# Second MLP, block 0: the first product done classically throughout, and the raw weights of the seven-product groups kept in two tiles that are loaded by quarters

## The chip, the cores and the metric

The kernel runs on one core of a Trainium2 chip. The metric is the device time of one execution in microseconds, as the median of several runs. One further execution was profiled; all rows below are from it.

## The reference

One inference step of a two-layer network on 640 tokens (512 latent and 128 context tokens) of width 1024. Each layer is a token mixer (pooling in layer 0, retention in layer 1) followed by a squared-ReLU MLP of hidden width 4096:

```python
def sq_relu_mlp(h, w1, w2):
    return jnp.square(jax.nn.relu(h @ w1)) @ w2

for i in range(DEPTH):                       # DEPTH = 2
    ...
    x = x + g_a * mix
    h = rmsnorm(x, norm_mlp_w[i]) * (1 + sc_m) + sh_m
    x = x + g_m * sq_relu_mlp(h, mlp_w1[i], mlp_w2[i])
```

The change touches `h @ w1` of both MLPs. All of it is float32.

## The kernel before, in words

**Precision.** A float32 matrix is split into two parts, high and low (`split`: ScalarE casts the high part, VectorE subtracts to get the low part). Each product is three matmuls (`mm3`): high by high, high by low, low by high. Activations lie transposed, 128 channels by 640 tokens per tile; a matmul takes 320 tokens, half of them. Tiles `h0h` to `h7l` are the MLP's input in its parts, `a` the hidden activations, `whi` and `wlo` the parts of weights, `wst` the raw weights as loaded. There are two buffers `wst` of 1024 KB and four pairs `whi`, `wlo`, so that splitting runs a few products ahead of TensorE.

**Blocks.** `mlp(i, ...)` goes over four blocks `b` of 1024 hidden channels. Each block is a first product (`h @ w1` for these channels, then ReLU, square, split: `hidden`) and a second product (`w2`, added into `x` by VectorE: `add_to_x`). In the second product, and in the classical first product, each of 8 column groups `n` takes 2 halves of tokens by 8 k-tiles by 3, 48 matmuls, 384 in all.

**Seven products.** For the blocks in `FAST` the first product is done in two halves of 512 columns, each by seven products of quarter matrices in place of eight (`fast`): 7 by 2 by 4 by 3, 168 matmuls in place of 192. The generator `seven` loads the raw weights of a half in two transfers of 1024 KB, makes the sums of weight quarters on VectorE (in place in `wst`) and yields seven split operands. The results gather in the PSUM banks `u`, `c11` and `c21`; bank `u` is used four times, and before TensorE may add the next product into it, ScalarE (`S.copy`) or VectorE (`kept`) must have read it.

**Sums of the activations.** The seven products need sums of quarters of the activations too: `quarters()` makes them, for each q of 4, with 12 VectorE instructions and 4 ScalarE casts on tiles of 128 by 320. They go to the tiles `tq`, and one of them overwrites the second half of tokens of `h0` to `h3`. It can therefore run only when no classical product needs these any longer. With `FAST[i] = (1, 2, 3)` the first MLP calls it at the start of block 1. In the second MLP `PART` has it run in block 0: there the columns 0 to 511 are done classically (`follow`, along with the norm that makes `h`), and the columns 512 to 1023 by seven products.

**Order.** The program is written in the order of the stages. A scheduler then merges the instructions of neighbouring stages into one fixed list for each engine (PE TensorE, DVE VectorE, ACT ScalarE, SP the queue that issues the loads), and each engine goes through its list strictly in order. A transfer is issued when its buffer is free of readers.

Of the kernel before, what the change touches and what calls it, by code (L numbers as in the profile page):

```python
# [9 lines left out]
F32 = mybir.dt.float32  # L10
# [55 lines left out]
PART = (False, True)  # L66
# [47 lines left out]
def hybrid_kernel(ctx: ExitStack, tc: tile.TileContext, x_prompt, x_sample, state_ret, c, c_ctx, w_ada, b_ada,  # L114
# [632 lines left out]
    def mlp(i, sq, norm, hm, step, along):  # L747

        with tc.tile_pool(name=f"hid{i}", bufs=1) as hid:
# [17 lines left out]
            def quarters():  # L767

                both = [hid.tile([128, 2048], F32, tag="both", name=nm("tq"), bufs=4).bitcast(F32R) for _ in range(4)]
                place = lambda q, t: [both[q][:, (2 * t + e) * HALF:(2 * t + e + 1) * HALF] for e in range(2)]  # L770
                part = lambda d, h: [z[:, HALVES[h]] for z in hm[d]]
                for q in range(4):
                    b11, b12, b21, b22 = (th() for _ in range(4))
                    for f, (d, h) in ((b12, (q, 1)), (b22, (q + 4, 1)), (b11, (q, 0)), (b21, (q + 4, 0))):
                        hi, lo = (z.bitcast(F32) for z in part(d, h))
                        V.tensor_tensor(f, hi, lo, ALU.add)
                    V.tensor_tensor(b22, b12, b22, ALU.subtract)
                    split(b22, *place(q, 1))
                    V.tensor_tensor(b12, b11, b12, ALU.subtract)
                    split(b12, *part(q, 1))  # L780
                    V.tensor_tensor(b11, b22, b11, ALU.subtract)
                    split(b11, *place(q, 0))
                    V.tensor_tensor(b21, b11, b21, ALU.add)
                    split(b21, *place(q, 2))
# [5 lines left out]
            def seven(src):  # L790


                (a11, a12), (a21, a22) = ([st[:, 4 * e:4 * e + 4] for e in range(2)] for st in (
                    load(src[:, o:o + 256], (8, 256)) for o in (0, 256)))
# [6 lines left out]
                yield split(a12, *parts())  # L801
# [3 lines left out]
                V.tensor_tensor(a12, a12, a11, ALU.add)  # L805
                V.tensor_tensor(a11, a11, a22, ALU.subtract)
                yield split(a11, *parts())
                yield split(a21, *parts())
                yield split(a12, *parts())
                yield split(a22, *parts())  # L810

            def fast(src, half, ops, take):

                ws = seven(src[:, half * 512:(half + 1) * 512])
# [30 lines left out]
            def fast_to_x(src, half, ops):  # L845


                ws = seven(src[:, half * 512:(half + 1) * 512])
                banks = {}

                def put(n, h, ps, gate):
                    t = th()
                    for j, cols in PARTS[h]:
                        S.activation(t[:, cols], ps[:, cols], AF.Copy, scale=gate[:, n, j:j + 1])
                    nc.gpsimd.dma_start(out=away[n][h], in_=t, accum_op=ALU.add)

                w = next(ws)
                for p, name in enumerate(("u", "c11", "u", "c21", "u", "u", "c21")):
                    after = next(ws, None)
                    for t in range(2):  # L860
# [7 lines left out]
                        put(*((n, 0), (n, 0), (n + 2, 0), (n + 2, 1), (n + 2, 1), (n, 1), (n + 2, 0))[p], ps,  # L868
                            minus if p in (2, 4) else mod[i][5])
                    w = after  # L870

            if BOTH[i]:
                away = [[dram.tile([128, HALF], F32, name=nm("away")) for _ in range(2)] for _ in range(KD)]
                minus = const.tile([128, KD, 2], F32, name="minus")
                V.tensor_scalar(minus, mod[i][5], -1.0, None, ALU.mult)

            def hidden_quarters():
# [6 lines left out]
                def places():  # L884
# [6 lines left out]
                    return ([[a[q + o][h] for q in range(4)] for o, h in ((0, 0), (4, 0))] +  # L891
                            [[sums[q, t] for q in range(4)] for t in range(2)] +
                            [[a[q + o][h] for q in range(4)] for o, h in ((0, 1), (4, 1))] +
                            [[sums[q, 2] for q in range(4)]])

                kept, have = {}, set()
                full = lambda z: z.bitcast(F32)

                def less(z, parts, op=ALU.subtract):

                    out = th()
                    for part in parts:
                        V.tensor_tensor(out, z, full(part), op)
# [3 lines left out]
                def take(n, h, ps):  # L907
# [10 lines left out]
                    if n < 4 and (q, 0) in have and (q, 1) in have:  # L918
# [4 lines left out]
                        else:  # L923
                            V.tensor_tensor(t, full(a[q][0][0]), f, ALU.subtract)
                            V.tensor_tensor(t, t, full(a[q][0][1]), ALU.add)
# [17 lines left out]
            for b in range(4):  # L943
# [29 lines left out]
                if b in FAST[i] or b == 0 and PART[i]:  # L973
                    if b == (0 if PART[i] else FAST[i][0]):
                        ops = quarters()
                    for half in range(b == 0, 2):
# [4 lines left out]
                    if b not in BOTH[i]:  # L981
                        get(2 * b + 1, 0)
                else:
                    for n in range(4 if b == 0 else 0, 8):
                        if n == FREE:
                            room[0] = room[1]
                        for h in range(2):
                            hidden(n, h, gemm([get(2 * b, n)], hm, h)[0])
                        step(STEPS[b][0][n])
# [388 lines left out]
```

## Time and profile before

| what | us |
|---|---|
| median of 3 runs | 1642.67 (1642.53 to 1644.59) |
| the profiled execution, its own time | 1642.23 |
| its span, first to last instruction | 1640.5 |
| TensorE busy in the span | 1585.3 (97%) |
| VectorE busy | 1175.7 (72%) |
| ScalarE busy | 730.3 (45%) |

1.7 us of the profiled execution lie around the span. Busy shares are means over stages with different limits, so they are to be read together with the idle time of TensorE by place.

### The profile page before, as it was taken

The page shows a single profiled execution, that of the slowest core. Times are in us where ns is not written, and L with a number is a line of the kernel's source. Part 1 is how long each engine was busy: PE and PEld are TensorE (multiplying, and loading weights), DVE is VectorE, ACT ScalarE, POOL GpSimd, SP SyncE. Part 2 cuts the span into 40 slices and gives each one's busy share as a digit, 9 for nine tenths or more (in the row PEclk, how much of TensorE's full clock was granted, in tenths as well). Part 3 has the DMA queues.
Part 4 walks back from the last instruction along what each step waited for, and adds up shares of the span by engine and source line. Part 5 has one row for each costly group of instructions (what it writes and reads, how often), then busy time and mean ns, then how long its engine had stood idle before and what let it go on. Part 6 is the DMA issues. An engine that isn't in the chain of part 4 may idle for free.

```text
span 1640.5 us, 24467 instructions
## 1 busy us (share of the span) xinstructions
PE 1585.3 (97%) x9873; PEld 1475.0 (90%) x9873; DVE 1175.7 (72%) x2267; ACT 730.3 (45%) x1347; POOL 11.9 (1%) x26
## 2 busy tenths in 40 slices
PE   6999999999999989999999999999969999999997
PEld 3559999999999978899889988989869999999997
DVE  7879996676765887875877688688885464554654
ACT  6747337246165354423432533353464272451640
POOL 0000000000000000000000000000000000000000
PEclk9999999999999999999999999999979999999999
DMA  9744233333314123233423332331104032131221
GB/s 358 240 153 142 93 101 114 104 117 103 103 52 155 56 78 120 87 104 102 131 75 114 94 102 77 128 112 66 56 1 129 27 121 86 52 103 52 92 77 65
DMA packets 137953, 169.81 MB, mean 104 GB/s; under 512 B 3512, under 2 KB 111472, under 8 KB 137840
## 3 DMA queue, kind: packets, MB, share of 16 engines
q1 hardware_dynamic: 134800, 161.28, 29.9%
q0 software_dynamic: 1312, 4.20, 0.8%
q10 hardware_dynamic: 1728, 2.78, 0.5%
q8 instruction: 77, 1.26, 0.3%
q14 instruction: 36, 0.29, 0.1%
HBM read 161.43 MB, written 6.82 MB: 103 GB/s over the span
## 4 chain that ended last, share of the span: by engine, by line
PE 79%; DVE 10%; ACT 5%; DMA 4%; issue 1%; ACTq 0%; DVEq 0%; SPq 0%; POOLq 0%
PE ps L212 22%; PE ps L213 22%; PE ps L214 22%; PE ps L287 3%; DMA wst<-in_mlp_w_dram 3%; PE ps L1124 2%; PE ps L1122 2%; PE ps L1123 2%; DVE wlo L152 2%; ACT whi L151 2%; DVE acc L393 1%; PE ps L635 1%; DMA wst<-in_ret_w_in_dram 1%; PE ps L469 1%; ACT t L487 0%
## 5 line engine op out<-in xcount | busy, mean ns | idle before, releaser
L151 ACT CAST whi<-wst 128x1024 fp32r<-128x1024 f32 x248 | 256.6, 1046 | 436.9 <-PE ps L213 222.3
L152 DVE TENSOR_TENSOR wlo<-wst,whi 128x1024 fp32r<-128x1024 f32 x248 | 300.3, 1221 | 127.1 <-ACT whi L151 127.0
L212 PE MATMUL ps<-a,whi 128*128 128x320 f32 x896 | 277.0, 310 | 1.4 <-ACT a L151 1.4
L213 PE MATMUL ps<-a,whi 128*128 128x320 f32 x896 | 277.3, 310 | 0.1
L214 PE MATMUL ps<-a,wlo 128*128 128x320 f32 x896 | 276.2, 309 | 0.0
L504 DVE SCALAR_TENSOR_TENSOR xall<-ps,mod,xall 128x320 f32<-128x320 f32 (+2 forms) x288 | 115.5, 435 | 170.3 <-PE ps L214 169.2
L213 PEld LDWEIGHTS ps<-a,whi 128*128 128x128 f32 x896 | 168.2, 188 | 2.3 <-DVE a L152 1.9
L212 PEld LDWEIGHTS ps<-a,whi 128*128 128x128 f32 x896 | 167.9, 188 | 1.9 <-ACT a L151 1.8
L214 PEld LDWEIGHTS ps<-a,wlo 128*128 128x128 f32 x896 | 168.0, 188 | 0.0
L393 DVE SCALAR_TENSOR_TENSOR acc<-wst,c,acc 128x256 f32<-128x256 f32 x336 | 137.1, 477 | 0.0
L212 PE MATMUL ps<-tq,whi 128*128 128x320 f32 x312 | 97.6, 313 | 15.3 <-issue 13.5
L213 PE MATMUL ps<-tq,whi 128*128 128x320 f32 x312 | 97.2, 312 | 0.0
L214 PE MATMUL ps<-tq,wlo 128*128 128x320 f32 x312 | 96.9, 312 | 0.0
L213 PE MATMUL ps<-A,whi 128*128 128x320 f32 x256 | 79.1, 310 | 0.0
L212 PE MATMUL ps<-A,whi 128*128 128x320 f32 x256 | 79.1, 312 | 0.0
L214 PE MATMUL ps<-A,wlo 128*128 128x320 f32 x256 | 78.4, 310 | 0.0
L212 PEld LDWEIGHTS ps<-tq,whi 128*128 128x128 f32 x312 | 59.4, 190 | 15.8 <-issue 13.7
L152 DVE TENSOR_TENSOR a<-t,a 128x320 fp32r<-128x320 f32 x128 | 61.7, 487 | 15.8 <-ACT a L151 15.5
L439 ACT ACTIVATE t<-xall 128x320 f32<-128x320 f32 x56 | 25.9, 470 | 84.1 <-DVE xall L504 84.0
L956 ACT ACTIVATE t<-t 128x320 f32<-128x320 f32 x128 | 60.4, 472 | 1.7
L213 PEld LDWEIGHTS ps<-tq,whi 128*128 128x128 f32 x312 | 59.4, 191 | 0.0
L214 PEld LDWEIGHTS ps<-tq,wlo 128*128 128x128 f32 x312 | 59.2, 190 | 0.0
(406 smaller groups left out, 3976.4 us busy)
## 6 DMA issues: line engine op xcount, KB each, us to landing
wst<-in_mlp_w_dram SPq DMA_DIRECT2D x64, 1024.0 KB, 5.3
wst<-in_w_ada_dram SPq DMA_DIRECT2D x46, 1024.0 KB, 5.3
wst<-in_ret_w_in_dram SPq DMA_DIRECT2D x24, 1024.0 KB, 5.2
wst<-in_ret_w_out_dram SPq DMA_DIRECT2D x8, 1024.0 KB, 5.0
t<-in_state_ret_dram SPq DMA_DIRECT2D x16, 256.0 KB, 5.5
out_dram<-t POOLq DMA_DIRECT2D x16, 256.0 KB, 2.9
xt<-in_x_sample_dram SPq DMA_DIRECT2D x4, 512.0 KB, 4.5
both<-in_w_ada_dram SPq DMA_DIRECT2D x2, 1024.0 KB, 6.3
```

What stands on the lines that cost most here:

```text
L151: S.copy(hi, src)
L152: sub.tensor_tensor(lo, src, hi.bitcast(F32), ALU.subtract)
L212: T.matmul(out, wh, ah, start=first, stop=False, skip_group_check=more)
L213: T.matmul(out, wh, al, start=False, stop=False, skip_group_check=more)
L214: T.matmul(out, wl, ah, start=False, stop=last, skip_group_check=more)
L287: T.matmul(pa, lhs[:, kk + k, :], z[:, k, :], start=first and k == 0 and j == 0, stop=last and k == 1 and j == len(w) - 1)
L393: V.scalar_tensor_tensor(acc[j], w[:, k], by, acc[j], ALU.mult, ALU.add)
L504: V.scalar_tensor_tensor(x, ps[:, cols], gate[:, d, j:j + 1], x, ALU.mult, ALU.add)
L956: S.activation(f, r, AF.Square)
L1122: T.matmul(out[i], hh[0], w[0][:, k, :], start=first, stop=False)
L1123: T.matmul(out[i], hh[1], w[0][:, k, :], start=False, stop=False)
L1124: T.matmul(out[i], hh[0], w[1][:, k, :], start=False, stop=last)
```

## The change

1. The second MLP's block 0 does all its columns classically, as the first MLP does. `PART` is gone, and the sums of the activations are made at the start of block 1 in both MLPs.
2. `quarters()` becomes `quarter(q)`: the same instructions, with the fourth sum (`b21`) begun later.
3. `seven` no longer takes a new pair of `wst` tiles for each half. A block holds one pair, `raw`, for both halves, and each half is loaded in four transfers of 512 KB, one for each quarter of the weights. A quarter's transfer waits only for the readers of that quarter. `raw.clear()` ends the block's hold.

The code for `BOTH` (`fast_to_x`, `hidden_quarters`) changes too, but `BOTH` is `((), ())` before and after, so nothing of it is in the program.

```diff
-PART = (False, True)
...
-                    if at < 64 and at // 16 not in (FAST, BOTH)[at // 8 % 2][i] and not (PART[i] and 4 <= at < 8):
+                    if at < 64 and at // 16 not in (FAST, BOTH)[at // 8 % 2][i]:
...
+            def quarter(q, last=True):
+
+                if not both:
+                    both.extend(hid.tile([128, 2048], F32, tag="both", name=nm("tq"), bufs=4).bitcast(F32R) for _ in range(4))
+                b12, b22, b11 = full(q, 1), full(q + 4, 1), full(q, 0)
+                V.tensor_tensor(b22, b12, b22, ALU.subtract)
+                split(b22, *place(q, 1))
+                if last:
+                    V.tensor_tensor(b12, b11, b12, ALU.subtract)
+                    split(b12, *part(q, 1))
+                V.tensor_tensor(b11, b22, b11, ALU.subtract)
+                split(b11, *place(q, 0))
+                b21 = full(q + 4, 0)
+                V.tensor_tensor(b21, b11, b21, ALU.add)
+                split(b21, *place(q, 2))
...
-            def seven(src):
+            raw = []
+
+            def seven(src, second):
...
-                (a11, a12), (a21, a22) = ([st[:, 4 * e:4 * e + 4] for e in range(2)] for st in (
-                    load(src[:, o:o + 256], (8, 256)) for o in (0, 256)))
+                if not raw:
+                    raw.extend(wst.tile([128, 2048], F32, tag="wst", name=nm("wst"), bufs=2).rearrange(
+                        "p (a b) -> p a b", a=8) for _ in range(2))
+                (a11, a12), (a21, a22) = ([st[:, 4 * e:4 * e + 4] for e in range(2)] for st in raw)
+                for z, e, o in ((a11, 0, 0), (a21, 0, 256), (a22, 1, 256), (a12, 1, 0)) if second else (
+                        (a11, 0, 0), (a12, 1, 0), (a21, 0, 256), (a22, 1, 256)):
+                    nc.sync.dma_start(out=z, in_=src[e * 512:(e + 1) * 512, o:o + 256].rearrange("(k p) n -> p k n", p=128))
...
-                if b in FAST[i] or b == 0 and PART[i]:
-                    if b == (0 if PART[i] else FAST[i][0]):
-                        ops = quarters()
-                    for half in range(b == 0, 2):
+                if b in FAST[i]:
+                    if b == FAST[i][0]:
+                        for q in range(4):
+                            (quarter_last if BOTH[i] else quarter)(q)
+                        ops = operands()
+                    for half in range(2):
                         fast(mlp_w1[i, :, blocks[b]], half, ops, hidden)
...
                     if b not in BOTH[i]:
+                        raw.clear()
                         get(2 * b + 1, 0)
```

**ScalarE, second MLP, block 0 before.** These rows follow each other in ScalarE's list where the seven products of block 0 begin. `tq` and `h0h` to `h3h` are the sums of the activations; `L831 COPY` reads the first product out of its bank `u`.

```order
L151 CAST tq_12203<-t_12207 128x320
L151 CAST tq_12203<-t_12209 128x320
L151 CAST tq_12204<-t_12230 128x320
L151 CAST h1h_11687<-t_12228 128x320
L151 CAST tq_12204<-t_12227 128x320
L151 CAST tq_12204<-t_12229 128x320
L151 CAST tq_12205<-t_12250 128x320
L151 CAST h2h_11689<-t_12248 128x320
L151 CAST tq_12205<-t_12247 128x320
L151 CAST tq_12205<-t_12249 128x320
L831 COPY t_12312<-ps_12299 128x320
L831 COPY t_12327<-ps_12314 128x320
```

The same list in the changed kernel, from the last casts of the sums (now beside the second product of block 0) to the first reads of bank `u` (block 1):

```order
L150 CAST tq_12960<-t_13023 128x320
L150 CAST h3h_11697<-t_13021 128x320
L150 CAST tq_12960<-t_13025 128x320
L150 CAST whi_12831<-wst_12772 128x1024
L150 CAST tq_12960<-t_13036 128x320
L150 CAST whi_13047<-wst_13041 128x1024
L150 CAST whi_13051<-wst_13041 128x1024
L150 CAST whi_13087<-wst_13041 128x1024
L150 CAST whi_13133<-wst_13041 128x1024
L867 COPY t_13068<-ps_13055 128x320
L150 CAST whi_13165<-wst_13042 128x1024
L867 COPY t_13083<-ps_13070 128x320
```

Before, the two copies stand behind ten casts of the sums shown here and two ahead of these. In the change all sixteen casts stand ahead of the four weight splits of block 1, and no copy of a bank stands among them.

**VectorE, second MLP, second product of block 0 in the change.** `xall<-ps` is `add_to_x`, which frees a bank; the rest are sums of the activations.

```order
L777 TENSOR_TENSOR t_12965<-h0h_11691,h0l_11692 128x320
L503 SCALAR_TENSOR_TENSOR xall<-ps_12487,mod_5_110,xall 128x320
L785 TENSOR_TENSOR t_12963<-t_12961,t_12963 128x320
L777 TENSOR_TENSOR t_12976<-h4h_11699,h4l_11700 128x320
L788 TENSOR_TENSOR t_12961<-t_12965,t_12961 128x320
L151 TENSOR_TENSOR tq_12957<-t_12963,tq_12957 128x320
L790 TENSOR_TENSOR t_12965<-t_12963,t_12965 128x320
L151 TENSOR_TENSOR h0l_11692<-t_12961,h0h_11691 128x320
L793 TENSOR_TENSOR t_12976<-t_12965,t_12976 128x320
L151 TENSOR_TENSOR tq_12957<-t_12965,tq_12957 128x320
L503 SCALAR_TENSOR_TENSOR xall<-ps_12513,mod_5_110,xall 128x192
```

The sums stand between the additions into `x`, a few to each addition.

**VectorE, second half of block 1 in the second MLP, before.** `wlo_13242` is the seventh split of the first half, `wlo_13324` the first of the second half; `L836` reads the fifth product's banks, which frees bank `u`; `L802` is the sum of the weight quarters a21 and a22.

```order
L152 TENSOR_TENSOR wlo_13242<-wst_13045,whi_13241 128x1024
L152 TENSOR_TENSOR wlo_13324<-wst_13319,whi_13323 128x1024
L836 TENSOR_TENSOR t_13182<-t_13182,ps_13055 128x320
L836 TENSOR_TENSOR t_13197<-t_13197,ps_13070 128x320
L802 TENSOR_TENSOR wst_13321<-wst_13321 128x1024
L152 TENSOR_TENSOR wlo_13328<-wst_13319,whi_13327 128x1024
```

The same place in the change (`L872` is `L836` before, `L830` is `L802`):

```order
L151 TENSOR_TENSOR wlo_13242<-wst_13042,whi_13241 128x1024
L151 TENSOR_TENSOR wlo_13324<-wst_13041,whi_13323 128x1024
L872 TENSOR_TENSOR t_13182<-t_13182,ps_13055 128x320
L830 TENSOR_TENSOR wst_13042<-wst_13042 128x1024
L872 TENSOR_TENSOR t_13197<-t_13197,ps_13070 128x320
L831 TENSOR_TENSOR wst_13041<-wst_13041,wst_13042 128x1024
L151 TENSOR_TENSOR a_12946<-t_13217,a_12945 128x320
```

The sum of a21 and a22, which needs the half's last transfer (a22), now stands between the two reads. It stands so in all six blocks of seven products.

## Rows read from the trace of the kernel before

**Rows 1.** Page, part 1: busy us, share of the span, instructions.

```profile
PE 1585.3 (97%) x9873; PEld 1475.0 (90%) x9873; DVE 1175.7 (72%) x2267; ACT 730.3 (45%) x1347; POOL 11.9 (1%) x26
```

**Rows 2.** Waits of PE by releaser: us in total, times, longest.

```profile
PE ps L212 <- issue: 13.5, 1, 13.5
```

**Rows 3.** Windows: stretch, length, busy by engine, granted clock, DMA share, GB/s.

```profile
1201.95:1248.35 46.40, 29.75 (x170) 28.58 (x169) 38.18 (x73) 27.50 (x56) 0.00 (x0) 0.78 0.14 46
1248.35:1304.80 56.45, 56.45 (x387) 56.33 (x386) 25.89 (x39) 10.56 (x15) 0.00 (x0) 1.00 0.24 75
...
181.65:238.90 57.25, 57.25 (x395) 57.24 (x394) 56.25 (x120) 16.66 (x27) 0.00 (x0) 1.00 0.34 109
```

**Rows 4.** Timeline of PE, 1201 to 1249: start, length, instruction, idle before, releaser.

```profile
1201.95 0.31 PE L212 MATMUL ps<-h0h,whi 128*128 128x320 f32 x1
...
1219.70 0.61 PE L212 MATMUL ps<-tq,whi 128*128 128x320 f32 x1 [13.47 <-issue]
...
1222.38 0.64 PE L214 MATMUL ps<-h4h,wlo 128*128 128x320 f32 x1 [1.28 <-DVE wlo L152]
...
1232.25 0.41 PE L212 MATMUL ps<-tq,whi 128*128 128x320 f32 x1 [1.80 <-ACT whi L151]
...
1248.35 0.31 PE L212 MATMUL ps<-a,whi 128*128 128x320 f32 x1
```

**Rows 5.** Timeline of ACT, 1201 to 1246.

```profile
1206.76 0.46 ACT L151 CAST tq<-t 128x320 fp32r<-128x320 f32 x1 [0.96 <-DVE t L777]
...
1219.18 0.75 ACT L831 COPY t<-ps 128x320 f32<-128x320 f32 x2
```

**Rows 6.** Timeline of DVE, 1201 to 1246.

```profile
1206.64 0.48 DVE L776 TENSOR_TENSOR t<-h1h,h1l 128x320 f32<-128x320 f32 x1
1207.04 0.48 DVE L779 TENSOR_TENSOR t<-t,t 128x320 f32<-128x320 f32 x1
```

**Rows 7.** Groups by line, DVE, 181.65 to 238.9 (first MLP): busy, mean ns, idle before.

```profile
L152 DVE TENSOR_TENSOR tq<-t,tq 128x320 fp32r<-128x320 f32 x12 | 5.8, 483 | 0.2 <-ACT tq L151 0.2
```

**Rows 8.** Timeline of PE: the waits within the blocks of seven products.

```profile
256.93 0.41 PE L212 MATMUL ps<-h4h,whi 128*128 128x320 f32 x1 [0.25 <-DVE t L836]
...
365.04 0.42 PE L212 MATMUL ps<-h4h,whi 128*128 128x320 f32 x1 [0.63 <-DVE t L836]
...
1453.94 0.42 PE L212 MATMUL ps<-h4h,whi 128*128 128x320 f32 x1 [0.47 <-DVE t L836]
```

**Rows 9.** Timeline of ACT and of DVE ahead of the last of these.

```profile
1451.18 1.05 ACT L151 CAST whi<-wst 128x1024 fp32r<-128x1024 f32 x1 [0.77 <-DMA wst<-in_mlp_w_dram]
...
1452.27 1.23 DVE L152 TENSOR_TENSOR wlo<-wst,whi 128x1024 fp32r<-128x1024 f32 x1 [3.63 <-ACT whi L151]
1453.41 0.88 DVE L836 TENSOR_TENSOR t<-t,ps 128x320 f32<-128x320 f32 x2
```

**Rows 10.** Windows of PE alone: the second block of seven products, and the sum of six.

```profile
346.65:396.89 50.24, 49.61 (x339) 1.00 0.32 105
...
sum 299.09, PE 297.63; mean PE 49.61
```

**Rows 11.** Timeline of SP, 1312 to 1332: both transfers of a second half.

```profile
1314.35 3.76 SPq L177 DMA_DIRECT2D wst<-in_mlp_w_dram  x2
```

**Rows 12.** Timeline of PE: the sixth product's two parts in that block's first half.

```profile
1322.52 0.41 PE L212 MATMUL ps<-h4h,whi 128*128 128x320 f32 x1
...
1324.38 0.31 PE L212 MATMUL ps<-h4h,whi 128*128 128x320 f32 x1
```

**Rows 13.** DMA issues: KB each, median us from issue to landing.

```profile
wst<-in_mlp_w_dram SPq DMA_DIRECT2D x64, 1024.0 KB, 5.3
...
t<-in_state_ret_dram SPq DMA_DIRECT2D x16, 256.0 KB, 5.5
...
xt<-in_x_sample_dram SPq DMA_DIRECT2D x4, 512.0 KB, 4.5
...
wb<-in_final_norm_w_dram SPq DMA_DIRECT2D x2, 256.0 KB, 3.5
```

More of the change, by code (lines that the diff above doesn't have):

```diff
@@ L762, in get @@
                     at = b * 8 + n + o
-                    if at < 64 and at // 16 not in (FAST, BOTH)[at // 8 % 2][i] and not (PART[i] and 4 <= at < 8):
+                    if at < 64 and at // 16 not in (FAST, BOTH)[at // 8 % 2][i]:
                         gets[at // 8](at % 8)
                 return gets[b](n)
[L767 to L778, printed above, removed]
+            both = []
@@ new lines, in place, with part, full @@
+            def place(q, t):
+                return [both[q][:, (2 * t + e) * HALF:(2 * t + e + 1) * HALF] for e in range(2)]
+            def part(d, h):
+                return [z[:, HALVES[h]] for z in hm[d]]
+            def full(d, h):
+                f = th()
+                V.tensor_tensor(f, *[z.bitcast(F32) for z in part(d, h)], ALU.add)
+                return f
+            def quarter(q, last=True):
[5 more added lines that the diff above has]
+                if last:
@@ L800, in seven @@
                 yield split(a11, *parts())
-                yield split(a12, *parts())
+                if not second:
+                    yield split(a12, *parts())
                 V.tensor_tensor(a21, a21, a22, ALU.add)
@@ L804, in seven @@
                 yield split(a11, *parts())
[L805 to L809, printed above, removed]
+                if second:
+                    yield split(a21, *parts())
+                    V.tensor_tensor(a21, a11, a12, ALU.add)
+                    V.tensor_tensor(a11, a11, a22, ALU.subtract)
+                    yield split(a11, *parts())
+                    yield split(a21, *parts())
+                    yield split(a12, *parts())
+                else:
+                    V.tensor_tensor(a12, a12, a11, ALU.add)
+                    V.tensor_tensor(a11, a11, a22, ALU.subtract)
+                    yield split(a11, *parts())
+                    yield split(a21, *parts())
+                    yield split(a12, *parts())
                 yield split(a22, *parts())
             def fast(src, half, ops, take):
-                ws = seven(src[:, half * 512:(half + 1) * 512])
+                ws = seven(src[:, half * 512:(half + 1) * 512], False)
                 banks, kept = {}, {}
@@ L845, in fast_to_x, with scaled @@
             def fast_to_x(src, half, ops):
-                ws = seven(src[:, half * 512:(half + 1) * 512])
-                banks = {}
-                def put(n, h, ps, gate):
+                ws = seven(src[:, half * 512:(half + 1) * 512], True)
+                banks, kept = {}, {}
+                gate = mod[i][5]
+                def scaled(n, h, ps):
                     t = th()
@@ L890, in places @@
                             hid.tile([128, HALF], F32R, tag=f"s{q}{t}{e}", name=nm("s")) for e in "hl"]
[L891 to L894, printed above, removed]
+                    of = lambda o, h: [a[q + o][h] for q in range(4)]
+                    up = lambda t: [sums[q, t] for q in range(4)]
+                    return [of(0, 0), up(0), of(0, 1), up(1), of(4, 1), of(4, 0), up(2)]
                 kept, have = {}, set()
-                full = lambda z: z.bitcast(F32)
+                plain = lambda z: z.bitcast(F32)
                 def less(z, parts, op=ALU.subtract):
                     out = th()
-                    for part in parts:
-                        V.tensor_tensor(out, z, full(part), op)
+                    for z2 in parts:
+                        V.tensor_tensor(out, z, plain(z2), op)
                         z = out
@@ L988, in mlp @@
                             hidden(n, h, gemm([get(2 * b, n)], hm, h)[0])
+                        if BOTH[i]:
+                            quarter(n - 4, False)
                         step(STEPS[b][0][n])
```

32 lines of the change are left out of this document (21 added, 11 removed).

## The prediction

> **What bounds the kernel now.** The first view is the page's list of engines: TensorE is busy for 97% of the span, the next engine for 72% [rows 1]. So time is gained only where TensorE waits, where it runs at a low clock, or where it is given less work. The second view lists what TensorE waited for. One wait stands out: 13.5 us, once, put down to "issue", which means that the profile names no releaser [rows 2]. The third is TensorE's timeline around it. It lies in the second MLP's block 0, in the half done by seven products, and two smaller waits follow in the same half [rows 4].
>
> That half begins at 1201.95 and the second product of the block at 1248.35, so it takes 46.40 us. To see what it should take I need the spacing of matmuls. The second product behind it is 384 matmuls in 56.45 us with TensorE busy throughout at the full clock, 1.00 in the row [rows 3]: 0.147 us each. The half's 168 matmuls are then worth 24.7 us, and 21.7 us are lost. The three waits are 13.47 + 1.28 + 1.80 = 16.55 us of it. The other 5.2 us are matmuls at the lower of the two clocks after the waits; the mean granted clock of the half is 0.78 [rows 3].
>
> Why does it wait? The matmul after the long wait is the third product's, which adds into bank `u`. ScalarE must first copy the first product out of this bank, and that copy starts at 1219.18, half a microsecond ahead of the matmul [rows 5]. In ScalarE's list the copies stand behind twelve casts of the activations' sums, and these wait in turn for VectorE, which works through the sums at one instruction per 0.40 us [rows 6]. For four q of 12 instructions that is 48 x 0.40 = 19 us of VectorE, with nothing for TensorE to do beside it. So the wait is the sums', although no row says so.
>
> **The change, part by part.**
>
> *The half done classically.* The columns 512 to 1023 take 192 matmuls in place of 168: 192 x 0.147 = 28.2 us where the half now takes 46.40. If TensorE doesn't wait, that is a gain of 18.2 us (21.7 lost now, less 24 more matmuls at 3.5 us). What the classical half needs is less than before: four weight splits in place of seven, no sums of weights, no reads of kept products. Nothing in it depends on the sums of activations.
>
> *The sums moved.* They now lie beside the second product of block 0, interleaved with its additions into `x`. VectorE is busy for 25.89 us of those 56.45, ScalarE for 10.56 [rows 3]. With 19 us more VectorE has 45 of 56, and ScalarE with 16 casts of 0.46 us [rows 5] has 18. The nearest row is the first MLP at the same stage, where the same 12 `tq` splits run [rows 7]: VectorE is busy there for 56.25 us of 57.25, with other work besides, and TensorE for all of 57.25 [rows 3]. So I cost the move at nothing. The cover is the second product, which uses `a` and bank by bank waits only for additions. If the cover were gone, the 13.5 us would be back.
>
> *The order within `quarter`.* The same 48 instructions, with the fourth sum later, beside the same covering stage: nothing in the first MLP either, by the same rows.
>
> *One pair of raw tiles, loaded by quarters.* This concerns all six blocks of seven products. Together they take 299.09 us [rows 10]; 6 x 336 x 0.147 is 296.4, so at most 2.7 us can be had from them. Of these, 1.35 us are three waits at one place: the sixth product's first matmul waits for VectorE's read of bank `u` [rows 8]. The rows ahead of the last one show the chain: ScalarE waits for the second half's first transfer, its cast and VectorE's split come late, and the read of `u` stands behind them in VectorE's list [rows 9]. In the change this transfer no longer waits for the sixth split, which is the last reader of its 1024 KB tile, but for the fourth, the last reader of quarter a11. That is two products of 24 x 0.147 = 3.5 us earlier, so it is there in time. I take 1.4 us as gained, with 0 and 2.7 as the bounds on this side.
>
> The other side is the sum of a21 and a22, which now stands between the two reads of `u` and waits for the half's last transfer. This is the added wait; behind it are the second read, and behind that the sixth product's second part on TensorE. In block 1 of the second MLP the last transfer is issued near 1317.7, just ahead of the end of the row of both at 1314.35 + 3.76 = 1318.1 [rows 11]; it waits for the seventh split, in the change too. The second part of the sixth product starts at 1324.38, or 1324.2 without the 0.2 us that the first part comes late [rows 12]. On VectorE 128 by 1024 takes 1.23 us [rows 9] and 128 by 320 takes 0.48 [rows 6], so the transfer must land by 1322.5, 4.8 us after its issue. What 512 KB take in this place no row shows. Bounds: 3.5 us for 256 KB, 5.3 for 1024 KB, 4.5 for 512 KB (four at once, at the program's start), and 5.5 for the slowest row, 256 KB of state [rows 13]. One at a time on an idle queue is nearest to a point between the first two, an estimate of 4.1 us. It then lands 0.7 us early and costs nothing. At 5.5 us it would be 0.7 us late in each of six blocks, 4.2 us in all.
>
> The Trainium skill speaks against this part. "DMA: Bandwidth & Descriptors" (section Bandwidth) has the rule to batch transfers to 1 MiB and more, since each carries a fixed cost of about 2 us. By its formula 512 KB take 2.0 + 1.2 = 3.2 us, an estimate from the page, under the 4.8 us that are allowed, and the sum stays as it is. The rows bear out the fixed cost in kind, since a quarter of the bytes takes two thirds of the time, and the queues have room: the DMA share in such a block is 0.32 [rows 10].
>
> *Twelve more issues on SP's list* cost nothing: SP computes nothing, and its issues wait for buffers.
>
> **The sum.** 1642.23 - 18.2 - 1.4 = 1622.6 for an execution like the profiled one. The median of the runs is 0.44 above that execution, so I predict 1623.0.
>
> **The rivals.**
>
> 1. *The quarters come late.* For it: the fixed part of a transfer's time in [rows 13] and the tight place in VectorE's list. Against it: 4.1 us against 4.8 allowed. The waits of [rows 8] then stay in another form, 0 to 4.2 us: 1642.23 - 18.2 + 4.2 + 0.4 gives up to 1628.6. The Trainium skill's rule on batching ("DMA: Bandwidth & Descriptors", section Bandwidth) points this way.
> 2. *Part of the stall is given back beside the second product.* The additions into `x` stand between sums that wait for ScalarE's casts and back, so a bank may come free late. For it: just this back and forth made the 13.5 us. Against it: in the first MLP the same mixture kept TensorE busy at all times. A third to a half of the 21.7 us back gives 1630 to 1634.
> 3. *Slower: the stall moves whole to the start of block 1 in the second MLP.* There the third product again needs `tq` of all four q. If the sums ran only after the last addition into `x`, TensorE would stand as it does now, with 3.5 us more matmuls: 1642.67 + 3.5 - 1.4 = 1644.8. It decides once more than 18.2 + 1.4 = 19.6 of the 21.7 us come back. Against it: beside the second product VectorE has 11 us to spare, and the order of the change has the casts ahead of block 1's splits.
> 4. *More gain.* All of the 2.7 us, and shorter waits elsewhere from a shifted schedule: 1618 to 1621.
>
> **How the numbers follow.** Likeliest case, 1620.5 to 1625: 0.70. Rival 1, 1625 to 1628.6: 0.12. Rival 2: 0.08. Rival 3: 0.04. Rival 4: 0.06. Range: from 1620 to 1628.6, which leaves out rivals 2 and 3 and most of 4, less than 2 in 10. A measurement of this kernel tells about 0.2% from no change, 3.3 us. All cases but rival 3 and the far end of rival 2 are faster by more: 0.94. Within 0.2%: 0.03. Slower: 0.03.
>
> **What would show it.** Right: no wait of TensorE over 2 us in the second MLP's block 0, its classical half of columns 512 to 1023 in about 28 us at a granted clock of 1.00, the `tq` splits beside the second product with TensorE busy there throughout, and the blocks of seven products at 49.3 to 49.8 us each with no wait on the read of `u`. Wrong in the part on quarters: a wait of TensorE at the second part of the sixth product, released by VectorE's read behind the sum of a21 and a22, in each second half. Wrong in the main part: a wait of several microseconds at the first `a` of block 0's second product, or at the first `tq` of block 1, or a half that stays near 46 us.

## The result and the profile after

The changed kernel took 1623.03 us in the median of four runs (1621.58 to 1625.39), the kernel before 1642.92 beside it: a ratio of 0.9878, with a 95% interval from 0.9861 to 0.9896. That is 19.9 us less, where 19.7 were forecast. The profiled execution took 1625.39 us, with a span of 1623.6.

The list of engines on the page, which answers to [rows 1]:

```profile
PE 1582.5 (97%) x9897; PEld 1475.1 (91%) x9897; DVE 1164.5 (72%) x2254; ACT 723.3 (45%) x1338; POOL 11.9 (1%) x26
```

The windows of block 0 in the second MLP, the half of columns 512 to 1023 and the second product, which answer to [rows 3]:

```profile
1204.46:1232.77 28.31, 28.31 (x196) 28.31 (x194) 11.36 (x16) 17.20 (x35) 0.00 (x0) 1.00 0.33 109
1232.77:1289.09 56.32, 56.32 (x387) 56.32 (x385) 42.33 (x83) 16.55 (x27) 0.00 (x0) 1.00 0.17 57
```

The half went from 46.40 to 28.31 us, with TensorE busy throughout at the full clock. The sums are now in the second product: VectorE is busy there for 42.33 us where it was for 25.89, and TensorE still doesn't wait.

The windows of TensorE alone over the six blocks of seven products, which answer to [rows 10]:

```profile
238.76:288.10 49.34, 49.34 (x339) 1.00 0.34 107
346.00:397.78 51.78, 49.80 (x339) 1.00 0.32 102
455.70:506.76 51.06, 49.54 (x339) 1.00 0.26 83
...
1395.06:1444.34 49.28, 49.28 (x339) 1.00 0.33 107
1500.87:1551.14 50.27, 49.54 (x339) 1.00 0.30 95
sum 301.10, PE 296.87; mean PE 49.48
```

Three blocks have come down to 49.28 to 49.37 us, which is what their matmuls take; three have become longer, and the sum is 2 us above that of before. TensorE's waits say why. The 13.5 us of [rows 2] are gone, and in the list there is a new line:

```profile
PE ps L211 <- DVE t L872: 4.2, 3, 2.0
```

`L872` is the read of bank `u` after the fifth product. All three waits stand at the first part of the sixth product in second halves, 43 to 45 us into the block. Of the waits of [rows 8] two stood in first halves, 18 us into the block, and nothing is left of them. The timeline ahead of the last of them, on SP's queue, ScalarE, VectorE and TensorE:

```profile
1534.93 0.37 SPq L176 DMA_DIRECT2D wst<-in_mlp_w_dram  x1
...
1541.24 1.05 ACT L150 CAST whi<-wst 128x1024 fp32r<-128x1024 f32 x1 [1.03 <-DMA wst<-in_mlp_w_dram]
...
1542.32 1.22 DVE L151 TENSOR_TENSOR wlo<-wst,whi 128x1024 fp32r<-128x1024 f32 x1 [3.83 <-ACT whi L150]
1543.46 0.88 DVE L872 TENSOR_TENSOR t<-t,ps 128x320 f32<-128x320 f32 x2
...
1544.00 0.41 PE L211 MATMUL ps<-h4h,whi 128*128 128x320 f32 x1 [0.73 <-DVE t L872]
```

The load at 1534.93 is the first of `w2`, 1024 KB, for the product behind this one. It takes the raw tile that the sixth split has just freed. Its own product begins at 1551, so TensorE has no hurry for it; but VectorE has its split in the list ahead of the read of `u`, and TensorE needs the read.

### The profile page after: what moved, and what is told of

Read it like the earlier page. It is cut to its first block, busy times and chain, and to the rows that moved or that the text cites. A ratio compares the mean times of both kernels' runs of the same rounds, so it can differ in the third digit from the quotient of the medians.

```text
span 1623.6 us, 24554 instructions
## 1 busy us (share of the span) xinstructions
PE 1582.5 (97%) x9897; PEld 1475.1 (91%) x9897; DVE 1164.5 (72%) x2254; ACT 723.3 (45%) x1338; POOL 11.9 (1%) x26
## 3 DMA queue, kind: packets, MB, share of 16 engines
q0 software_dynamic: 1312, 4.20, 0.8%
## 4 chain that ended last, share of the span: by engine, by line
PE 86%; DVE 6%; ACT 4%; DMA 3%; issue 1%; DVEq 0%; ACTq 0%; SPq 0%; POOLq 0%
PE ps L211 24%; PE ps L212 24%; PE ps L213 24%; PE ps L286 3%; PE ps L1179 2%; PE ps L1177 2%; PE ps L1178 2%; DMA wst<-in_mlp_w_dram 1%; DVE wlo L151 1%; DVE acc L392 1%; ACT whi L150 1%; PE ps L634 1%; PE ps L397 1%; PE ps L468 1%; ACT t L486 0%
## 5 line engine op out<-in xcount | busy, mean ns | idle before, releaser
L151 DVE TENSOR_TENSOR wlo<-wst,whi 128x1024 fp32r<-128x1024 f32 x245 | 296.7, 1220 | 129.0 <-ACT whi L150 128.5
L212 PE MATMUL ps<-tq,whi 128*128 128x320 f32 x288 | 89.0, 309 | 0.0
L213 PE MATMUL ps<-tq,wlo 128*128 128x320 f32 x288 | 89.0, 309 | 0.0
L211 PE MATMUL ps<-tq,whi 128*128 128x320 f32 x288 | 89.0, 309 | 0.0
L150 ACT CAST a<-t 128x320 fp32r<-128x320 f32 x128 | 58.4, 456 | 1.3
L211 PEld LDWEIGHTS ps<-tq,whi 128*128 128x128 f32 x288 | 54.1, 188 | 0.0
L212 PEld LDWEIGHTS ps<-tq,whi 128*128 128x128 f32 x288 | 54.1, 188 | 0.0
```

The costliest lines, as they stand in the source:

```text
L150: S.copy(hi, src)
L151: sub.tensor_tensor(lo, src, hi.bitcast(F32), ALU.subtract)
L211: T.matmul(out, wh, ah, start=first, stop=False, skip_group_check=more)
L212: T.matmul(out, wh, al, start=False, stop=False, skip_group_check=more)
L213: T.matmul(out, wl, ah, start=False, stop=last, skip_group_check=more)
```

## The experiments

**The yardstick.** The changed kernel again, in the first group of runs.

> The changed kernel once more, as the yardstick of this group. Theory: 1621.5 to 1625.5, as in its four runs so far; the second MLP's block 0 has no wait of TensorE over 1 us and its half of columns 512 to 1023 takes about 28.3 us at a granted clock of 1.00. The waits of TensorE for the read of bank u stand at the first part of the sixth product in second halves, each behind a load of w2 that took 5.5 us or longer; which blocks they fall in may differ from run to run if the loads are late by chance, and stays as it was if the lateness is fixed by the program.

Measured: 1622.45 us (1621.06 to 1624.88), before 1643.22, ratio 0.9878 (0.9863 to 0.9893). Two of the three waits came back, 1.45 us in the first MLP's block 3 and 0.74 us in the last block; the one of 1.98 us did not. The six blocks take 298.60 us in this profile.

**Block 0 alone**, an edit of the kernel before:

```diff
-PART = (False, True)
+PART = (False, False)
```

> The kernel before with block 0 of the second MLP done classically throughout, and nothing else of the change: the raw weights still come in tiles of 1024 KB. Theory (the whole gain is the stall of 21.7 us less 24 matmuls of 0.147 us = 18.2 us, and the quarters are worth within 2 us of nothing): 1622.5 to 1626.5, with the half of columns 512 to 1023 at 28.3 us and the small waits of 0.25 to 0.63 us at the first part of the sixth product back in first halves. Rival (the quarter loads are a part of the gain): 1628 or above, with the difference to the changed kernel found in the six blocks of seven products.

Measured: 1627.82 us (1626.44 to 1628.81), ratio 0.9905 (0.9891 to 0.9918), so 15.4 us less than before and 5.4 more than the changed kernel in the same group. That misses the theory's range by over 1 us and falls just short of the rival's. In place the gain is whole: the half takes 28.33 us. It is given back in the blocks of seven products; the last block and the sum of the six in the windows of TensorE:

```profile
1501.07:1554.05 52.98, 51.20 (x338) 0.97 0.28 90
sum 303.49, PE 299.77; mean PE 49.96
```

The last block took 49.55 us before. TensorE's timeline in it has the same wait as in the changed kernel, and longer:

```profile
1545.37 0.42 PE L212 MATMUL ps<-h4h,whi 128*128 128x320 f32 x1 [1.78 <-DVE t L836]
...
1546.10 0.47 PE L212 MATMUL ps<-h5h,whi 128*128 128x320 f32 x1
```

So the theory that the quarters are worth nothing beside block 0 fell: in this group the changed kernel has two waits for the read of `u`, 2.2 us together, and block 0 alone five, 3.5 us together.

**The quarters alone**, an edit of the changed kernel:

```diff
+PART = (False, True)
...
-                if b in FAST[i]:
-                    if b == FAST[i][0]:
+                if b in FAST[i] or b == 0 and PART[i]:
+                    if b == (0 if PART[i] else FAST[i][0]):
...
-                    for half in range(2):
+                    for half in range(b == 0, 2):
```

> The changed kernel with block 0's half of columns 512 to 1023 by seven products again, as before: of the change only the quarter loads and the order within the sums are left. Theory (these are worth within 2 us of nothing, and the sums stall TensorE wherever they stand alone): 1640.5 to 1645, with one wait of 12 to 15 us ahead of the third product of that half. Rival (quarters let the weights of that half come sooner and shorten the stall): below 1638, with a wait under 10 us.

Measured: 1640.97 us (1637.97 to 1642.75, 11 runs), ratio 0.9985 (0.9977 to 0.9994): 2.3 us less than before. The stall is there as it was, in the list of TensorE's waits:

```profile
PE ps L212 <- issue: 13.1, 1, 13.1
...
PE ps L212 <- DVE t L873: 2.3, 2, 1.5
```

The second line is the read of `u`. Its two waits, 0.73 and 1.53 us, stand in second halves of the first MLP's blocks 2 and 3; in the second MLP there is none, and its three blocks of seven products take 49.28 us each (before 49.62, 50.06 and 49.55). So the wait in the first MLP's block 3, which the kernel before doesn't have, comes with the quarters, whatever the second MLP's block 0 does. The theory holds, and with 2.3 against 15.4 us the two parts of the change together give more (20.8 us in this group) than the sum of each alone.

**Three quarters of the sums left out**, an edit of the kernel before. In the second MLP the sums are made for one q and used for all four; every matmul, copy and load is still there.

```diff
-                place = lambda q, t: [both[q][:, ...
+                place = lambda q, t: [both[0 if i == 1 else q][:, ...
...
-                for q in range(4):
+                for q in range(1 if i == 1 else 4):
```

> The kernel before with the sums of the activations of the second MLP made for one q of four alone, and used for all four; three quarters of these sums are left out, and the matmuls, copies and loads are all there. Theory (the stall of 21.7 us in block 0 is the 48 instructions of VectorE with their casts, ahead of ScalarE's first copy of bank u): 36 of 48 instructions fewer at 0.40 us are 14.4 us less ahead of the copy, so the wait of 13.5 us all but goes, and so does most of the low clock behind it: 1624 to 1630, the half under 34 us. Rival (the wait is for something else, a load of weights or their splits): the wait stays over 8 us and the time over 1636.

Measured: 1628.96 us (1624.95 to 1629.03), before 1643.63, ratio 0.9904 (0.9888 to 0.9920): 14.7 us less, where 14.4 were worked out from 36 instructions of 0.40 us. The profiled execution is the one of 1624.95, 4 us under the others. The window of the half, and ScalarE's timeline in it:

```profile
1200.80:1230.22 29.42, 25.95 (x170) 24.65 (x169) 23.46 (x37) 21.84 (x44) 0.00 (x0) 1.00 0.22 73
```

```profile
1204.54 0.76 ACT L831 COPY t<-ps 128x320 f32<-128x320 f32 x2
1205.60 0.46 ACT L151 CAST tq<-t 128x320 fp32r<-128x320 f32 x1 [0.31 <-DVE t L777]
```

The half takes 29.42 us in place of 46.40, and the copy that frees bank `u` now runs ahead of the casts, not behind them as in [rows 5]. This shows what the prediction had only inferred: the wait put down to "issue" was the sums'. The edit changed two things at once, the number of the sums and the copy's place in the list; both belong to that cause, and this run doesn't part them.

**The sums made twice**, an edit of the changed kernel, second MLP only:

```diff
                         for q in range(4):
-                            (quarter_last if BOTH[i] else quarter)(q)
+                            if i == 1:
+                                quarter(q, False)
+                            quarter(q)
```

> The changed kernel with 10 of the 12 VectorE instructions of each q, and 3 of its 4 casts, run twice in the second MLP beside the second product of block 0: 40 x 0.40 = 16 us more of VectorE in a stage of 56.3 us in which it is busy for 42.3. Theory (sums beside the second product are hidden as long as VectorE has room; the additions into x free the banks in time): only what overflows shows, 42.3 + 16 - 56.3 = 2 us, plus waits of the same order where sums stand between additions: 0 to 8 us over the changed kernel, 1623 to 1631. Rival (the sums are not hidden, and their time shows where they stand): 16 us over, 1637 to 1641.

Measured: 1622.95 us (1620.92 to 1624.73), ratio 0.9877 (0.9859 to 0.9894), no different from the changed kernel. The window of block 0's second product:

```profile
1228.77:1285.09 56.32, 56.32 (x386) 56.32 (x385) 54.69 (x121) 21.45 (x39) 0.00 (x0) 1.00 0.18 57
```

VectorE is busy for 54.69 of 56.32 us, 12.4 more than in the changed kernel, and TensorE doesn't wait. By the page the 40 instructions add 16.2 us (1180.7 against 1164.5); another 3.1 us are found in block 1 behind this window, into which other work of VectorE has moved (36.01 us busy there where it was 32.89), and TensorE doesn't wait there either (49.28 us). The sums are hidden even when VectorE is all but full.

**The quarters paired otherwise in the raw tiles**, an edit of the changed kernel:

```diff
-                (a11, a12), (a21, a22) = ([st[:, 4 * e:4 * e + 4] for e in range(2)] for st in raw)
+                (a11, a21), (a12, a22) = ([st[:, 4 * e:4 * e + 4] for e in range(2)] for st in raw)
```

> The changed kernel with the quarters paired otherwise in the two raw tiles: a11 with a21 and a12 with a22. The first tile is then free after the fifth split in place of the sixth, so the first 1024 KB of w2 are issued one product earlier, 24 x 0.147 = 3.5 us. Theory (the new waits of 0.73 to 1.98 us at the sixth product of second halves come from this load landing late, with VectorE's read of bank u standing behind the split of it): these waits go, 4.2 us in the profiled execution, and the time is 1619 to 1622, 1 to 4 us under the changed kernel of this group. Rival (the waits are VectorE's own work, or the load is late whenever it is issued): waits and time unchanged, within 1 us of the changed kernel.

Measured: 1621.99 us (1621.20 to 1623.22), ratio 0.9871 (0.9857 to 0.9884). The waits in the second halves are gone but for one of 0.36 us, as the theory has it; the sum of the six blocks in the windows of TensorE:

```profile
sum 297.67, PE 296.20; mean PE 49.37
```

But the median is only 0.5 us lower, which these runs can't tell from nothing and which fits the rival's "within 1 us". In the first MLP's block 2 a new wait has come in a first half. VectorE's and TensorE's timeline there:

```profile
366.24 1.23 DVE L830 TENSOR_TENSOR wst<-wst,wst 128x1024 f32<-128x1024 f32 x1 [2.12 <-DMA wst<-in_mlp_w_dram]
367.38 0.48 DVE L872 TENSOR_TENSOR t<-t,ps 128x320 f32<-128x320 f32 x1
...
367.91 0.42 PE L211 MATMUL ps<-h4h,whi 128*128 128x320 f32 x1 [1.11 <-DVE t L872]
```

This is rival 1 as the prediction described it: the sum of a21 and a22 waits for the half's last quarter, and the second read of `u` and the second part of the sixth product stand behind it.

**A further raw tile for the first load of `w2`**, first attempt, on the changed kernel and on block 0 alone:

```diff
-                    raw[i // 2] = load(src[:, ...], (k, 2 * wide))
+                    raw[i // 2] = load(src[:, ...], (k, 2 * wide),
+                                       own() if own and not i else None)
...
+            own = lambda: hid.tile([128, 2048], F32, tag="own", name=nm("own"), bufs=1)
...
-                gets.append(weights(mlp_w2[i, cols], (wsp, hid) if cols is blocks[3] else (wsp,)))
+                gets.append(weights(mlp_w2[i, cols], (wsp, hid) if cols is blocks[3] else (wsp,),
+                                    own=None if cols is blocks[0] else own))
```

> The changed kernel with one more raw tile of 1024 KB in the MLPs, which takes the first load of w2 in the blocks of seven products, so that this load waits for no reader of the half before. Theory (the waits at the sixth product of second halves come from this load alone): no wait of TensorE over 0.3 us in the second halves, the six blocks at 49.3 to 49.5 us each, 295.7 to 297.5 together against 298.6 and 301.1 in the two profiles of the changed kernel, and a time 1.5 to 4 us under the changed kernel of this group, 1618.5 to 1621. Rival (the load isn't what VectorE waits for, or the wait moves to the next load, since the second load of w2 now takes the place of the first): within 1 us of the changed kernel, with a wait of like size a little later.

> Block 0 classical alone, with loads of 1024 KB as before, and the further raw tile for the first load of w2. Theory (what block 0 alone falls short of the changed kernel, 5.4 us, is late loads in both halves: the second half's first tile, which quarters cure, and w2's first tile, which the further tile cures): the waits in second halves go, those of 0.2 to 0.7 us in first halves stay, and the time is 2 to 4 us under block 0 alone, 1624 to 1626. Rival (the quarters give something else than loads in time): within 1 us of block 0 alone.

> The changed kernel, as the yardstick of this group and for a third profile. Theory (late loads fall by chance): 1621 to 1625, with one to three waits at the sixth product of second halves, not all at the places of the two profiles so far.

> Block 0 classical alone once more, for a second profile. In the first one the last block of seven products took 52.98 us, with one wait of 1.78 us and matmuls at the lower clock behind it. Theory (this wait and the clock behind it belong to the place, since the load of w2 is late there in most executions): 1626 to 1629, with the last block over 51 us again. Rival (it was chance): the last block under 50.5 us and the profiled execution at 1624 to 1626.

Measured: 1622.41 and 1626.41 us, beside 1623.48 for the changed kernel and 1627.71 for block 0 alone. The edit did nothing: `get` asks for the second group of weights first, so the condition on the first never held, and the instructions are those of the two kernels without it. The four runs are therefore repeats. The changed kernel has four medians by now, 1622.41 to 1623.48, and its six blocks take 301.10, 298.60, 299.44 and 298.69 us in the four profiles. Block 0 alone has 1626.41 to 1627.82, with 303.49, 301.91 and 300.90 us. The wait in the last block is in all seven (0.61 to 0.90 us in the one, 1.13 to 1.78 in the other), so it belongs to the place. The wait in the first MLP's block 3 is in all four profiles of the changed kernel (1.43 to 1.52 us) and in none of block 0 alone; that in the first MLP's block 2 comes and goes. The last block of block 0 alone did take 50.88 us the second time, between what was expected of chance and of the place; the low clock behind the wait did not come again.

**The same, with the load really in the further tile** (the edit with `i < 2` for `not i`):

> The changed kernel with one more raw tile of 1024 KB in the MLPs for the first load of w2 in the blocks of seven products, this time with the load really placed in it: it is issued before the block begins. Theory (the waits at the sixth product of second halves come from this load alone): no wait of TensorE over 0.3 us in the second halves, the six blocks at 49.3 to 49.5 us each, 295.7 to 297.5 us together against 298.6 to 301.1 in the profiles of the changed kernel, and 1618.5 to 1621 for the median, 1.5 to 4 us under the changed kernel. Rival (the load isn't what VectorE waits for, or the wait moves to the next load of w2): 1622 to 1625, with a wait of like size a little later.

> Block 0 classical alone, loads of 1024 KB as before, and the further raw tile for the first load of w2. Theory (what block 0 alone falls short of the changed kernel, 4 to 5 us, is late loads in both halves, and the further tile cures those in second halves): the waits of 0.2 to 0.7 us in first halves stay, those in second halves go, and the time is 1.5 to 4 us under block 0 alone, 1623.5 to 1626. Rival (the shortfall lies with the loads of 1024 KB in first halves): 1626 to 1628.

Measured: 1618.41 us (1617.78 to 1620.42) for the changed kernel with the tile, before 1643.55, ratio 0.9851 (0.9836 to 0.9865); 1623.06 us (1620.89 to 1623.92) for block 0 alone with it, ratio 0.9875 (0.9859 to 0.9892). Beside the means of the medians so far (1622.84 and 1627.31, from other groups) both gain 4 to 5 us, a little beyond the theory's ranges. The windows of TensorE of the first: one block still has a wait (0.36 us), the other five take 49.28.

```profile
452.31:502.21 49.90, 49.54 (x339) 1.00 0.27 85
...
sum 296.30, PE 295.94; mean PE 49.32
```

The timeline of ScalarE and VectorE at the place shown above for the changed kernel:

```profile
1535.06 1.05 ACT L150 CAST whi<-own 128x1024 fp32r<-128x1024 f32 x1 [1.19 <-PE ps L213]
...
1536.14 1.22 DVE L151 TENSOR_TENSOR wlo<-own,whi 128x1024 fp32r<-128x1024 f32 x1 [2.23 <-ACT whi L150]
1537.28 0.48 DVE L875 TENSOR_TENSOR t<-t,ps 128x320 f32<-128x320 f32 x1
```

The cast no longer waits for a DMA but for TensorE to free its `whi`, and the read follows in time. In block 0 alone with the tile, TensorE's waits of 0.73, 0.45 and 0.21 us in first halves are still there, and there is one of 0.55 us in a second half: what the quarters cure and what the tile cures are different loads. The changed kernel with the tile is the fastest version here; each of its four runs is below each of the 16 runs of the changed kernel.

## Why the prediction was right, and where it was not

*The half done classically*, 18.2 us forecast: 46.40 to 28.31 is 18.1 (one profile each). The sums were the cause (with three quarters of them left out 14.7 us were gone), and nothing of the stall returned.

*The sums moved*, priced at nothing: right, and rivals 2 and 3 with it. The sums made twice cost nothing either. The spare time of VectorE, which the prediction put at 11 us, was nearer to 14.

*The quarters.* The step that failed is the reading of [rows 9]: "ScalarE waits for the second half's first transfer". The wait that these rows lead to, at 1453.94, stands 43 us into its block, in the second half; the transfer is not one of the half's own but the first of `w2`, as in the changed kernel's timeline above. The prediction's mechanism holds for the two waits in first halves, 0.25 and 0.63 us: in the four profiles of the changed kernel no wait on the read of `u` is left there. The load of `w2`, though, is issued after the sixth split in both kernels, so the quarters can't bring it sooner by much, and in the change TensorE waits behind it in three places. Two are the last block and, in two of the four profiles, the first MLP's block 2, where the load itself took longer (see the last section). The third is the first MLP's block 3, and there the load landed no later than before: issued at 491.08 it landed 41.4 us into the block before, issued at 491.32 it landed 41.1 us into it in the change. What differs is VectorE's list. Before:

```profile
496.21 0.48 DVE L836 TENSOR_TENSOR t<-t,ps 128x320 f32<-128x320 f32 x1
497.53 1.23 DVE L152 TENSOR_TENSOR wlo<-wst,whi 128x1024 fp32r<-128x1024 f32 x1 [0.83 <-ACT whi L151]
498.67 0.48 DVE L836 TENSOR_TENSOR t<-t,ps 128x320 f32<-128x320 f32 x1
```

In the change, with TensorE's wait:

```profile
497.94 1.22 DVE L151 TENSOR_TENSOR wlo<-wst,whi 128x1024 fp32r<-128x1024 f32 x1 [0.99 <-ACT whi L150]
499.08 0.88 DVE L872 TENSOR_TENSOR t<-t,ps 128x320 f32<-128x320 f32 x2
...
499.62 0.41 PE L211 MATMUL ps<-h4h,whi 128*128 128x320 f32 x1 [1.52 <-DVE t L872]
```

Before, the first read of `u` stood ahead of the split of `w2`, and TensorE didn't wait; in the change both reads stand behind it. The prediction looked at what the new list does to the sum of a21 and a22, not at this split.

So the sign "no wait on the read of `u`" was not met, and the 1.4 us that were to be gained in the six blocks became 0.4 us lost (mean of the four profiles 299.46 against 299.09). That can't be told from nothing: the first MLP's three blocks, which have the same lists before, in block 0 alone and with a quarter of the sums, took 149.82 to 150.90 us in those five profiles. Measured against block 0 alone, the quarters do take 2.6 us off the six blocks (302.10 to 299.46, means of three and four profiles) and 4 to 5 us off the median. All of the 2.6 us lie in the second MLP (151.45 to 148.86); in the first the three blocks take 150.65 and 150.60, the waits of first halves having been traded for the one in block 3. With its seven products in block 0 the second MLP's blocks took 149.23 us before and 147.84 with the quarters alone (one profile each). So block 0 done classically costs 1 to 2 us in these later blocks, which the prediction did not see, and the quarters give that back.

*The sum* came out within 0.1 us of the median, closer than its terms, and that is luck: the quarters fell 1.8 us short, and 1.4 us that nobody forecast made up for it. In profiles: 18.1 gained and 0.4 lost make 17.7; the mean of the four profiled executions (1625.39, 1621.06, 1623.55, 1622.70) is 1623.18, 19.1 under 1642.23. The other 1.4 us lie in stretches that the prediction gave no price: the second product of block 3 in the first MLP (59.20 us before, 59.00, 57.82, 58.46 and 58.73 in the four; a wait for ScalarE's cast of `a`, 1.36 us before, was 1.16, none, 0.61 and 0.88) and the stretch from the start of the last second product to the end (73.24, against 72.44 to 72.51). What shortened them was not followed up.

*Rival 1.* A load of 512 KB took 3.8 us where 4.1 were estimated and 4.8 allowed, by the page's part on DMA issues:

```profile
wst<-in_mlp_w_dram SPq DMA_DIRECT2D x40, 1024.0 KB, 5.3
wst<-in_mlp_w_dram SPq DMA_DIRECT2D x48, 512.0 KB, 3.8
```

It occurred in one place in the changed kernel, and there in small: in the first half of the first MLP's block 2, where the second half's weights come in, the last of their four transfers took 4.75 us, and the sum of a21 and a22 waited for it:

```profile
363.84 1.23 DVE L830 TENSOR_TENSOR wst<-wst 128x1024 f32<-128x1024 f32 x1 [1.00 <-DMA wst<-in_mlp_w_dram]
```

TensorE lost 0.3 us by it at most, and less in the other three profiles; the run with other pairs, where the same sum waited 2.12 us and TensorE 1.11, shows how near it is. The Trainium skill's fixed cost for each transfer ("DMA: Bandwidth & Descriptors", section "Anatomy of one DMA — SWDGE (gpsimd) path", where its formula stands too) agrees in kind: half the bytes take 72% of the time. That formula was fitted to transfers issued by GpSimd, and these are issued by SP. Its 3.2 us was too low, the measured 3.8 decides.

## What to carry to other kernels

Where a wait names no releaser, read the list of the engine that must free the bank: what stands ahead of the freeing instruction there is the cause, and leaving out a part of it tests that cheaply. Work of this kind is best put beside a stage in which the engines that do it have room, even at the price of more matmuls. When a load is made to come in time, look which load is next in the same list: a split that nobody needs yet holds up the read behind it, and a raw tile of its own for that load was worth 4 us here. Compare the lists of all engines before and after, since a change in the loads can also reorder the work behind them.

## What was unexpected of the hardware

**Instruction fetches and loads.** A DMA queue that the profile calls "instruction" fetches now and then a packet of 0.02 MB, which takes one of the 16 engines for 0.9 to 1.9 us in the last block of seven products. There the first load of `w2` took 5.0 to 5.2 us in the four kernels where no such packet fell into it (the kernel before, the quarters alone, the other pairs, a quarter of the sums), and 6.1 to 7.1 us in the eight profiles where one did (the changed kernel four times, block 0 alone three times, the sums twice). The DMA view of the load in the changed kernel, with the columns packets, MB and share, and median us to landing:

```profile
q8 instruction: 1, 0.02, 0.9%
q14 instruction: 1, 0.01, 0.4%
issues: line engine op xcount, KB each, median us to landing
wst<-in_mlp_w_dram SPq DMA_DIRECT2D x2, 1024.0 KB, 6.3
```

0.9% of 16 engines over the 6.3 us of the load are 0.9 us of one engine. The same load in the kernel before, without a line of an instruction queue:

```profile
q1 hardware_dynamic: 1257, 1.27, 74.9%
issues: line engine op xcount, KB each, median us to landing
wst<-in_mlp_w_dram SPq DMA_DIRECT2D x2, 1024.0 KB, 5.2
```

The packet comes at the same place in each execution of a kernel: 35.5 to 37.9 us into the last block where block 0 is classical, 40.1 to 40.8 where it has its seven products. That fits a fetch that goes by the place in the program, which the change of block 0 shifted onto the load; it would explain what block 0 alone lost in the last block. The numbers agree: the changed kernel has 78 such packets to 9897 matmuls and as many weight loads, one for about 254 of them, and 24 more matmuls in block 0, 24 x 0.147 = 3.5 us of TensorE's list, should bring a place in the list that much earlier into the block, where it came 3.7 us earlier (means 40.5 and 36.8). That such a packet lengthens a load is borne out by the other loads: of the 1024 KB loads of MLP weights that ran with no other transfer beside them, in all 14 profiles, 69 without such a packet took 4.9 to 5.5 us, and nine of 36 with one took 6.0 to 6.7. It also tells when the wait in the first MLP's block 2 comes: the packet starts 0.5 us after the issue of the load where the wait is 1.98 us and 0.1 to 0.2 us after it where it is 0.79 and 0.73 (the quarters alone), and at most 0.1 us after it in the three profiles without a wait (the changed kernel twice, the sums twice). Still no run moved the fetch by itself, so that the fetch is the cause is argued and not shown, and it is not all: in the first MLP's block 3 such a packet falls late into the load, which takes 5.1 to 5.6 us with it, and the wait there comes from the place of the split in VectorE's list, as told above.

**A wait and the clock.** Two waits of like size at the same place of a block cost differently: 1.98 us made the changed kernel's block 51.78 us at a granted clock of 1.00, 2.5 above 49.28; 1.78 us in block 0 alone made it 52.98 at 0.97, 3.7 above, since matmuls behind it ran at the lower of the two clocks. What decides between the two these profiles don't show.
